# Two pairs of tokens instead of one group of four in the one-hot rows of the dense gates

## The chip, the core and the metric

The kernel runs on one core of a Trainium2 chip. The metric is device microseconds of one execution; lower is better. The unchanged kernel was run three times for its time, and once more with the hardware profiler.

## What is computed

The reference is two transformer blocks over 512 tokens of width 1024. The part that matters here is the PEER layer of the first block: eight heads each choose 16 of 16,384 experts for a token, and each chosen expert contributes `gate * v_e * gelu(u_e . x)`.

```python
def peer(h, wq, k1, k2, u, v):
    ...
    top_s, top_c = lax.top_k(cand, PEER_TOPK)
    expert = (i1[top_c // 16] * PEER_N_KEYS + i2[top_c % 16])      # 128 choices a token
    gate = jax.nn.softmax(top_s, axis=-1)
    ...
    act = gelu(einsum("pd,ped->pe", xb, u[eb]))
    return einsum("pe,ped->pd", gb * act, v[eb])
```

## The kernel before

For 448 of the 512 tokens (`DT`) the kernel does not gather experts. It computes `gelu(u_e . x)` for all 16,384 experts, multiplies by a dense table of gates that is zero where a token did not choose the expert, and multiplies by all `v_e`. The expert number is written as `a * 128 + b`, so a token's gates are a 128x128 matrix over (b, a), and that matrix is a product of one-hot matrices: for the 128 choices of one token (they lie on the partitions) row `b` one-hot is the stationary operand, row `a` one-hot times the gate is the moving operand, and TensorE sums over the choices. The gate is split into two f16 parts, so each token takes two accumulating products of 128x128 by 128x128.

Three tiles carry this, all f16. `hb` holds for each choice and token four numbers: a, b and the two gate parts. `iob` holds the numbers 0 to 127, each repeated. `oh` holds four tokens' one-hot rows: index 0 is a, index 1 is b, 2 and 3 are a's one-hot times the gate parts. For each group of four tokens VectorE makes `oh` in two instructions of 128x1024: an `is_equal` of `iob` with `hb` (L917, i = 0) and a product (L917, i = 2). Then TensorE makes eight products `pg` (L923), each with its own weight load, whose operands are the columns of one token in `oh`. In `oh` before, the four tokens are the innermost index, so one token's 128 elements stand 8 bytes apart. ScalarE copies the four tokens' result to `stg` (L924), and after 32 tokens `stg` goes to DRAM (`Gd`, 2 MB each, L926). There are 112 such groups, 896 products, and `oh` has two buffers.

This work is a generator, `router()`, whose steps are woven into the loop `for a in range(P)` over 128 tiles of experts. Each turn of that loop loads and splits a tile of `u` (`getw`: DMA to `wr`, ScalarE's cast to `wh` at L123, VectorE's rest `wl` at L124) and runs 24 products `pu` of 448 columns (L140 to L142). The loop also draws on `ada_step` (L264, VectorE rows over weights of the second block) and on `own_dots` (L945, VectorE dot products of gathered rows). How many steps of a generator come in a turn is set by the numbers they yield; every engine then executes its instructions in the order of the program. The dense-gate part takes some 42 turns and ends at a = 121; six turns later the loop over `peer_v` (`pvv`) follows.

Of the kernel before, what the change touches and what calls it, by code (L numbers as in the profile page):

```python
# [11 lines left out]
F16 = mybir.dt.float16  # L12
# [3 lines left out]
AF = mybir.ActivationFunctionType  # L16
OP = mybir.AluOpType
# [4 lines left out]
P = 128  # L22
D = 1024
T = 512
# [52 lines left out]
def body(tc, I, O, dbg=None):  # L77
    nc = tc.nc
    V, S, TE, G, SP = nc.vector, nc.scalar, nc.tensor, nc.gpsimd, nc.sync
    es = ExitStack()  # L80

    def pool(name, bufs=1, space=None, side=None, ctx=es):
        kw = {}
        if space is not None:
            kw["space"] = space
        if side is not None:
            kw["side"] = side
        return ctx.enter_context(tc.tile_pool(name=name, bufs=bufs, reuse_waits="tile", **kw))
# [24 lines left out]
    iota = ca[:, CA["iota"]:CA["iota"] + 128]  # L113
# [185 lines left out]
    with ExitStack() as e1:  # L299
# [121 lines left out]
        wk = pool("wk1", ctx=er)  # L421
# [6 lines left out]
        ps = gps.tile([P, 512], F32, tag="g", name="lps")[:, :4]  # L428
# [19 lines left out]
        def proj(n_ctx=True, lat=True):  # L448
            done = first.pop(0) if first else None
            wh, wl = done[0] if done else getw1(P)  # L450
            out = []
            if done:
                out.append(done[1])
            elif lat:
                ps = mm.tile([P, 512], F32, tag="mm", name="pj")
                mm_tiles([(ps, wh, wl)], H)
                out.append(ps)
            if n_ctx:
                pc = mm.tile([P, 512], F32, tag="mm", name="pjc")[:, :C]
                mm_tiles([(pc, wh, wl)], HC)  # L460
                out.append(pc)
            return out
# [181 lines left out]
        for p_ in range(4):  # L644
            vl, vc = proj_v()
            for hh in range(2):
                h = 2 * p_ + hh
                kf, lg = [], []
                for d in range(2):
                    _, f = sig_tile(proj(), Z_, KL)  # L650
                    i = d * 8 + h
# [20 lines left out]
        wk = pool("wk1g", ctx=er)  # L672
# [7 lines left out]
        for hh, at, n in ((H, 0, T), (HC, T, C)):  # L680
            ps = mm.tile([P, 512], F32, tag="mm", name="grp")[:32, :n]
# [3 lines left out]
        for h in range(4):  # L685
# [4 lines left out]
            for d in range(2):  # L690
                y_ = wk.tile([P, N2], F32, tag=KL[0], name="gz", bufs=KL[1])
                for at, n in ((0, T), (T, C)):
                    ps = mm.tile([P, 512], F32, tag="mm", name="gkp")[:, :n]
# [25 lines left out]
        wk = pool("wk1b", ctx=ey)  # L719
        yh = wk.tile([P, 2, 16, T], F32R, name="yh1")  # L720
        for i in range(16):
            t = wk.tile([P, T], F32, tag="yl", name="yl", bufs=2)
            SP.dma_start(t, ysd[i])
            split(yh[:, 0, i], yh[:, 1, i], t)
        for i in range(16):
            ps, = proj(n_ctx=False)
# [9 lines left out]
        for n in range(KT):  # L736
            acc = []
            ada_step(wk, row1, 4)
            for br in range(2):
# [3 lines left out]
                ps = mb.tile([P, 512], F32, tag="mm", name="br")  # L743
# [14 lines left out]
        for n in range(KT):  # L758
            wh, wl = getw1(P)
            ps = mb.tile([P, 512], F32, tag="mm", name="wo")  # L760
# [31 lines left out]
    with ExitStack() as e1:  # L792
# [3 lines left out]
        wk = wk2 = pool("wk2", ctx=e1)  # L796
# [6 lines left out]
        wk = wk2  # L803
# [4 lines left out]
        eall = wk.tile([P, 4, P], F32, name="eall")  # L808
        gall = wk.tile([P, 4, 8, 16], F32, name="gall")
        abg = rp.tile([P, T], F32, name="abg")  # L810
        hb = wk.tile([P, 4, T], F16, name="hb")
        iob = wk.tile([P, P, 4], F16, name="iob")
        hrow = rp.tile([P, 1024], F32, name="hrow")
        V.tensor_copy(iob, iota[:, :, None].to_broadcast([P, P, 4]))
        rows = {}
        for (i, j) in RANKS:
            rows[i] = rows.get(i, 0) + 1
# [9 lines left out]
        def router():  # L827
            for h in range(8):
                vs, xs = [], []
                for half in range(2):  # L830
                    wh, wl = getw(I["wq"][h * 2 + half], P)
                    ps = mm.tile([P, 512], F32, tag="mm", name="pq")
# [5 lines left out]
                    ps = gps.tile([P, 512], F32, tag="g", name="ps")  # L838
# [19 lines left out]
                for w, src in enumerate((vs, xs)):  # L858
                    at = 0
                    for i in range(8):  # L860
                        n = rows[i]
# [40 lines left out]
            for w, src in enumerate((abf[:, 0], abf[:, 1], gall.rearrange("p m h i -> p m (h i)"))):  # L902
                tp = gps.tile([P, 512], F32, tag="g", name="tpg")
                for m in range(4):
                    TE.transpose(tp[:, m * P:(m + 1) * P], src[:, m], ident)
                S.activation(abg, tp, AF.Copy, scale=2.0 ** 15) if w == 2 else S.copy(hb[:, w], tp)

            S.copy(hb[:, 2], abg)
            V.tensor_tensor(hb[:, 3], abg, hb[:, 2], op=OP.subtract)
            yield 0.7  # L910
            for tb in range(DT // TB):
                stg = wk.tile([P, P, TB], F32, tag="stg", name="stg", bufs=2)
                for t4 in range(TB // 4):
                    t = tb * TB + t4 * 4
                    oh = wk.tile([P, 4, P, 4], F16, tag="oh", name="oh", bufs=2)
                    for i in (0, 2):
                        V.tensor_tensor(oh[:, i:i + 2], (oh[:, 0] if i else iob)[:, None].to_broadcast([P, 2, P, 4]),  # L917
                                        hb[:, i:i + 2, None, t:t + 4].to_broadcast([P, 2, P, 4]),
                                        op=OP.mult if i else OP.is_equal)
                    ps = gps.tile([P, 512], F32, tag="g", name="pg").rearrange("p (t a) -> p t a", t=4)  # L920
                    for j in range(4):
                        for i in range(2):
                            TE.matmul(ps[:, j], oh[:, 1, :, j], oh[:, 2 + i, :, j], start=i == 0, stop=i == 1)  # L923
                    S.activation(stg[:, :, t4 * 4:t4 * 4 + 4], ps.rearrange("p t a -> p a t"), AF.Copy, scale=2.0 ** -15)  # L924
                    yield 1.4
                SP.dma_start(Gd[tb], stg.rearrange("p a t -> p (a t)"))  # L926
# [22 lines left out]
        NG, GA = 16, 8  # L949
        ready = [0]  # L950
        lane, mine = router(), own_dots()
        WORK = 8 * 36.2 + 4.7 + 1.4 * DT / 4 + 1.3 * NSL
        spent = n_own = 0.0
# [3 lines left out]
        for a in range(P):  # L957
            if first:
                ps = first.pop(0)[0]
            else:  # L960
                wh, wl = getw(I["peer_u"][a], P)
                ps = mm.tile([P, 512], F32, tag="mm", name="pu")[:, :DT]
                mm_tiles([(ps, wh, wl)], Hd)
            t = gl.tile([P, DT], F32, tag="gel", name="gel", bufs=4)
# [52 lines left out]
    with ExitStack() as e1:  # L1017
        mm = pool("mm2b", 6, PSUM, ctx=e1)
        wk = pool("wk3", ctx=e1)
# [4 lines left out]
        for g in range(NG):  # L1024
# [15 lines left out]
            for j in range(KT):  # L1040
                wh, wl = getw(I["peer_v"][g * KT + j], P)
                ps = mm.tile([P, 512], F32, tag="mm", name="pvv")[:, :DT]
# [3 lines left out]
                while n_own < NSL + LAG and n_own < (NSL + LAG) * (g * KT + j + 1) / ((NG - 2) * KT):  # L1046
                    if n_own < NSL:
                        vs.append(fetch(wk, I["peer_vr"], n_own, LAG))
                    if n_own >= LAG:
                        n = n_own - LAG  # L1050
# [64 lines left out]
    for l in range(2):  # L1115
# [20 lines left out]
        wk = pool(f"wk6{l}", side="right", ctx=ea)  # L1136
# [163 lines left out]
        for hf in range(2):  # L1300
            ws = [getw(next2(), 256) for _ in range(2)]
            for uu, nt, o0 in ((UC, 2, 0), (U, 4, 2)):
                for m in range(nt):
                    ps = mm.tile([P, 512], F32, tag="mm", name="pr2")[:, :256]
# [7 lines left out]
        for m in range(6):  # L1312
            if m % 2 == 0:
                ps2 = sps.tile([P, 1024], F32, tag="sp", name="pvb")
            ps = ps2[:, m % 2 * 512:m % 2 * 512 + 512]
# [6 lines left out]
        for t_ in range(4):  # L1322
            st_ = [ptile("kb_s", F32R) for _ in range(2)]
            ps = sps.tile([P, 1024], F32, tag="sp", name="pkb")
# [6 lines left out]
        for t_ in range(6):  # L1331
            if t_ % 3 == 0:
                uqs = getw(I["uq"][l, t_ // 3], P, 768)
            ps = sps.tile([P, 1024], F32, tag="sp", name="pqb")
            for a0 in range(0, NQ, 512):
                a1 = min(NQ, a0 + 512)
                for k in range(2):
                    i = (t_ % 3) * 2 + k
# [161 lines left out]
        for bi, (q0, m) in enumerate(blocks):  # L1500
# [4 lines left out]
            for g in range(2):  # L1505
                ws = []
                for r in range(4):
# [3 lines left out]
                    for c0, c1 in ((0, 256), (256 + lo_ * P, 256 + hi_ * P)):  # L1511
                        while c0 < c1:
                            n = min(c1 - c0, 512 - at % 512)
# [35 lines left out]
        with ExitStack() as e2:  # L1549
            mm = pool(f"mm6{l}", 8, PSUM, ctx=e2)  # L1550
            wk = pool(f"wk7{l}", side="right", ctx=e2)
            for n_ in range(3):
# [5 lines left out]
                for jp in range(4):  # L1558
                    wh, wl = getw(I[f"wb_{l}"][n_ * 4 + jp], P)
                    for jj in range(2):  # L1560
                        j = jp * 2 + jj
                        gt = wk.tile([P, NQ], F32, tag="yt", name="gt2", bufs=6)
                        SP.dma_start(gt, gd2[n_ * 8 + j, :, :NQ])
                        for a0, n in spans:
                            ps = mm.tile([P, 512], F32, tag="mm", name="pb")[:, :n]
# [37 lines left out]
        with ExitStack() as e2:  # L1603
            mm = pool(f"mm7{l}", 6, PSUM, ctx=e2)
            for j in range(KT):
                wh, wl = getw(I[f"wo_{l}"][j], P)
                for hh, a0, n, w in toks:
                    ps = mm.tile([P, 512], F32, tag="mm", name="pwo")[:, :n]
# [10 lines left out]
        with ExitStack() as e2:  # L1619
# [5 lines left out]
            wk = pool(f"wk8{l}", ctx=e2)  # L1625
# [262 lines left out]
```

## Time and profile before

| | |
|---|---|
| median of 3 runs | 4973.27 us (4970.96 to 4980.0) |
| profiled execution | 4975.9 us, span 4974.1 us |
| TensorE busy | 4832.7 us (97%) |
| VectorE busy | 3295.3 us (66%) |
| ScalarE busy | 1968.7 us (40%) |
| mean granted TensorE clock | 0.989 |
| dense gates (first to last `pg`) | 1514.7 to 1828.4 us of the span |

The profiled execution is 2.6 us above the median. The shares are means over many stages; the dense gates are 6% of the span, and only this stretch runs the changed instructions in number.

### The profile page before, as it was taken

The numbers are of one execution on the slowest core, as the hardware profiler recorded it, in microseconds if no ns is written. First come the engines' busy times: TensorE is split into PE (matmuls) and PEld (weight loads), VectorE is DVE, ScalarE is ACT, GpSimd is POOL, SyncE is SP. The second block draws the span as 40 slices with busy tenths as digits, with TensorE's granted clock in tenths as the row PEclk, the third lists the DMA queues.
The fourth block names the chain that finished last, engine by engine and source line by source line (L and its number), as shares of the span: only waits on it lengthen the run. The fifth ranks groups of instructions, "written<-read, shape, count | busy, mean of one in ns | idle before, by whom it ended". The sixth has DMA issues, their size and how long they took to land.

```text
span 4974.1 us, 67442 instructions
## 1 busy us (share of the span) xinstructions
PE 4832.7 (97%) x26062; PEld 4111.5 (83%) x26062; DVE 3295.3 (66%) x6062; ACT 1968.7 (40%) x3214; POOL 345.7 (7%) x352
## 2 busy tenths in 40 slices
PE   7999999999999999999999999999999999999999
PEld 6888888788888988999988768888888886677887
DVE  7665556688888866777658773268655568726655
ACT  4544445332233432333345553224222455533433
POOL 0000000001111103333000100000000001100000
PEclk9999999999999999999999999999999999999999
DMA  4211117656667778777534532444432245245332
GB/s 163 62 52 54 56 51 245 212 176 203 218 210 249 262 254 305 265 263 271 163 118 119 136 83 96 143 146 132 143 116 71 72 138 138 69 140 180 91 96 85
DMA packets 236676, 752.08 MB, mean 151 GB/s; under 512 B 27458, under 2 KB 55618, under 8 KB 233796
## 3 DMA queue, kind: packets, MB, share of 16 engines
q1 hardware_dynamic: 193156, 580.00, 35.8%
q0 software_dynamic: 43200, 167.79, 11.2%
q8 instruction: 204, 3.34, 0.3%
q14 instruction: 116, 0.95, 0.1%
HBM read 619.09 MB, written 123.35 MB: 149 GB/s over the span
## 4 chain that ended last, share of the span: by engine, by line
PE 84%; DVE 8%; DMA 4%; ACT 3%; issue 2%; POOL 0%; DVEq 0%; ACTq 0%; SPq 0%; POOLq 0%
PE pj L140 6%; PE pj L141 6%; PE pj L142 6%; PE pvv L140 4%; PE pup L140 4%; PE pvv L141 4%; PE pvv L142 4%; PE pup L142 4%; PE pup L141 4%; PE pu L142 3%; PE pu L140 3%; PE pu L141 3%; PE tp L1230 3%; PE pg L923 2%; PE pdn L140 2%; PE pdn L141 2%
## 5 line engine op out<-in xcount | busy, mean ns | idle before, releaser
L123 ACT CAST wh<-wr 128x1024 fp32r<-128x1024 f32 (+4 forms) x660 | 679.1, 1029 | 1610.8 <-PE pvv L141 370.1
L124 DVE TENSOR_TENSOR wl<-wr,wh 128x1024 fp32r<-128x1024 f32 (+4 forms) x660 | 788.7, 1195 | 678.4 <-ACT wh L123 661.7
L142 PE MATMUL pu<-H,wl 128*128 128x448 f32 x1024 | 382.8, 374 | 12.4 <-DVE wl L124 12.4
L140 PE MATMUL pvv<-W,wh 128*128 128x448 f32 x1024 | 376.5, 368 | 15.3 <-ACT W L123 15.3
L140 PE MATMUL pu<-H,wh 128*128 128x448 f32 x1024 | 383.4, 375 | 5.0 <-ACT H L223 3.0
L142 PE MATMUL pvv<-W,wl 128*128 128x448 f32 x1024 | 376.4, 368 | 3.5 <-DVE wl L124 3.5
L141 PE MATMUL pu<-H,wh 128*128 128x448 f32 x1024 | 378.9, 370 | 0.0
L140 PE MATMUL pup<-U,wh 128*128 128x512 f32 (+1 forms) x1056 | 374.1, 355 | 3.2 <-ACT U L223 3.0
L141 PE MATMUL pvv<-W,wh 128*128 128x448 f32 x1024 | 376.2, 368 | 0.1
L141 PE MATMUL pup<-U,wh 128*128 128x512 f32 (+1 forms) x1056 | 374.3, 355 | 0.0
L142 PE MATMUL pup<-U,wl 128*128 128x512 f32 (+1 forms) x1056 | 374.1, 354 | 0.2 <-DVE wl L124 0.2
L140 PE MATMUL pj<-U,wh 128*128 128x512 f32 (+1 forms) x672 | 267.6, 398 | 0.0
L141 PE MATMUL pj<-U,wh 128*128 128x512 f32 (+1 forms) x672 | 267.4, 398 | 0.0
L142 PE MATMUL pj<-U,wl 128*128 128x512 f32 (+1 forms) x672 | 265.5, 395 | 0.0
L140 PEld LDWEIGHTS pup<-U,wh 128*128 128x128 f32 x1056 | 200.0, 190 | 32.8 <-ACT U L223 4.2
L142 PEld LDWEIGHTS pup<-U,wl 128*128 128x128 f32 x1056 | 199.7, 189 | 28.8 <-DVE wl L124 0.6
L141 PEld LDWEIGHTS pup<-U,wh 128*128 128x128 f32 x1056 | 199.9, 189 | 27.7 <-DVE U L224 0.3
L142 PEld LDWEIGHTS pu<-H,wl 128*128 128x128 f32 x1024 | 195.4, 191 | 32.4 <-DVE wl L124 15.7
L140 PEld LDWEIGHTS pvv<-W,wh 128*128 128x128 f32 x1024 | 193.7, 189 | 31.4 <-ACT W L123 15.7
L140 PEld LDWEIGHTS pu<-H,wh 128*128 128x128 f32 x1024 | 195.7, 191 | 23.1 <-ACT H L223 4.5
L142 PEld LDWEIGHTS pvv<-W,wl 128*128 128x128 f32 x1024 | 193.8, 189 | 19.8 <-DVE wl L124 4.1
L141 PEld LDWEIGHTS pu<-H,wh 128*128 128x128 f32 x1024 | 195.1, 191 | 17.3 <-DVE H L224 0.4
(507 smaller groups left out, 11925.5 us busy)
## 6 DMA issues: line engine op xcount, KB each, us to landing
wr<-in_w_dram SPq DMA_DIRECT2D x146, 512.0 KB
wr<-in_peer_u_dram SPq DMA_DIRECT2D x128, 512.0 KB
wr<-in_peer_v_dram SPq DMA_DIRECT2D x128, 512.0 KB
wa<-in_ada2T_dram SPq DMA_DIRECT2D x96, 512.0 KB
wr<-in_up_dram SPq DMA_DIRECT2D x88, 512.0 KB
geld<-gel SPq DMA_DIRECT2D x128, 224.0 KB
Gd<-stg SPq DMA_DIRECT2D x14, 2048.0 KB
gt<-Gd POOLq DMA_DIRECT2D x32, 896.0 KB, 8.4
```

The costliest lines, as they stand in the source:

```text
L123: S.copy(hi, src)
L124: V.tensor_sub(lo, src, r32(hi))
L140: TE.matmul(ps, ah, bh, start=start, stop=False)
L141: TE.matmul(ps, ah, bl, start=False, stop=False)
L142: TE.matmul(ps, al, bh, start=False, stop=stop)
L923: TE.matmul(ps[:, j], oh[:, 1, :, j], oh[:, 2 + i, :, j], start=i == 0, stop=i == 1)
L1230: TE.transpose(tp[:, m * P:(m + 1) * P], w_[:, c0:c0 + P], ident)
```

## The change

In `oh` the four tokens of a group become two pairs: the order of the indices was (kind, n, token) and is now (kind, pair, n, token in the pair). A token's 128 elements then stand 4 bytes apart. `iob` repeats each number twice instead of four times, and `hb` is stored as (group of four tokens, kind, token), so that the two pairs of one or two kinds follow one another. The two VectorE instructions of a group keep their 1024 elements a partition; the innermost run of the `hb` operand is two elements instead of four. The products and their number are the same.

```diff
-        hb = wk.tile([P, 4, T], F16, name="hb")
-        iob = wk.tile([P, P, 4], F16, name="iob")
+        hb = wk.tile([P, T // 4, 4, 4], F16, name="hb")
+        iob = wk.tile([P, P, 2], F16, name="iob")
...
-        V.tensor_copy(iob, iota[:, :, None].to_broadcast([P, P, 4]))
+        V.tensor_copy(iob, iota[:, :, None].to_broadcast([P, P, 2]))
...
-                S.activation(abg, tp, AF.Copy, scale=2.0 ** 15) if w == 2 else S.copy(hb[:, w], tp)
-
-            S.copy(hb[:, 2], abg)
-            V.tensor_tensor(hb[:, 3], abg, hb[:, 2], op=OP.subtract)
+                S.activation(abg, tp, AF.Copy, scale=2.0 ** 15) if w == 2 else S.copy(hb[:, :, w], tp.rearrange("p (g t) -> p g t", t=4))
+
+            ag4 = abg.rearrange("p (g t) -> p g t", t=4)
+            S.copy(hb[:, :, 2], ag4)
+            V.tensor_tensor(hb[:, :, 3], ag4, hb[:, :, 2], op=OP.subtract)
...
-                    oh = wk.tile([P, 4, P, 4], F16, tag="oh", name="oh", bufs=2)
+                    oh = wk.tile([P, 4, 2, P, 2], F16, tag="oh", name="oh", bufs=2)
                     for i in (0, 2):
-                        V.tensor_tensor(oh[:, i:i + 2], (oh[:, 0] if i else iob)[:, None].to_broadcast([P, 2, P, 4]),
-                                        hb[:, i:i + 2, None, t:t + 4].to_broadcast([P, 2, P, 4]),
-                                        op=OP.mult if i else OP.is_equal)
+                        row = hb[:, t // 4, i:i + 2].rearrange("p w (u v) -> p (w u) v", v=2)
+                        dst = oh[:, i:i + 2].rearrange("p w u n v -> p (w u) n v")
+                        if i == 0:
+                            V.tensor_tensor(dst, iob[:, None].to_broadcast([P, 4, P, 2]),
+                                            row[:, :, None].to_broadcast([P, 4, P, 2]), op=OP.is_equal)
+                        else:
+                            V.tensor_tensor(oh[:, 2:4], oh[:, 0, None].to_broadcast([P, 2, 2, P, 2]),
+                                            hb[:, t // 4, 2:4].rearrange("p w (u v) -> p w u v", v=2)[:, :, :, None].to_broadcast([P, 2, 2, P, 2]),
+                                            op=OP.mult)
...
-                            TE.matmul(ps[:, j], oh[:, 1, :, j], oh[:, 2 + i, :, j], start=i == 0, stop=i == 1)
+                            TE.matmul(ps[:, j], oh[:, 1, j // 2, :, j % 2], oh[:, 2 + i, j // 2, :, j % 2], start=i == 0, stop=i == 1)
```

No engine's instructions change place. This is VectorE where the dense gates begin, before the change (`aj,sdot` are the dot products of `own_dots`, `aj,ac` those of `ada_step`):

```order
L917 TENSOR_TENSOR oh<-iob,hb 128x1024 x2
L124 TENSOR_TENSOR wl<-wr,wh 128x1024
L909 TENSOR_TENSOR hb<-abg,hb 128x512
L917 TENSOR_TENSOR oh<-oh,hb 128x1024 x2
L945 SCALAR_TENSOR_TENSOR aj,sdot<-ut,hrow 128x1024
L917 TENSOR_TENSOR oh<-iob,hb 128x1024 x2
L917 TENSOR_TENSOR oh<-oh,hb 128x1024 x2
L264 SCALAR_TENSOR_TENSOR aj,ac<-wa,rows_u_8239 128x1024
```

And the same place with the change:

```order
L922 TENSOR_TENSOR oh<-iob,hb 128x1024 x2
L124 TENSOR_TENSOR wl<-wr,wh 128x1024
L910 TENSOR_TENSOR hb<-abg,hb 128x128x4
L925 TENSOR_TENSOR oh<-oh,hb 128x1024 x2
L953 SCALAR_TENSOR_TENSOR aj,sdot<-ut,hrow 128x1024
L922 TENSOR_TENSOR oh<-iob,hb 128x1024 x2
L925 TENSOR_TENSOR oh<-oh,hb 128x1024 x2
L264 SCALAR_TENSOR_TENSOR aj,ac<-wa,rows_u_8239 128x1024
```

Only line numbers and the shape of the `hb` operand differ; on TensorE, GpSimd and SyncE no operand shape differs either, on ScalarE the three copies to `hb` do, on VectorE also the copy to `iob`.

## Rows read from the trace of the kernel before

**Rows 1.** The page, its busy times and its chain that ended last.
```profile
PE 4832.7 (97%) x26062; PEld 4111.5 (83%) x26062; DVE 3295.3 (66%) x6062; ACT 1968.7 (40%) x3214; POOL 345.7 (7%) x352
...
PE 84%; DVE 8%; DMA 4%; ACT 3%; issue 2%; POOL 0%; DVEq 0%; ACTq 0%; SPq 0%; POOLq 0%
```

**Rows 2.** Busy time by stretch, dense gates: stretch, us, engines, PEclk, DMA share, GB/s.
```profile
1515.00:1555.00 40.00, 40.00 (x247) 35.95 (x245) 33.68 (x53) 17.19 (x27) 5.50 (x4) 1.00 0.70 240
...
1675.00:1715.00 40.00, 40.00 (x247) 36.09 (x246) 32.13 (x52) 15.89 (x25) 4.15 (x4) 1.00 0.80 278
...
1795.00:1829.00 34.00, 34.00 (x214) 30.45 (x213) 26.34 (x38) 15.36 (x24) 0.00 (x0) 1.00 0.57 202
sum 314.00, PE 314.00 PEld 281.73 DVE 256.08 ACT 127.09 POOL 29.01; mean PE 39.25 PEld 35.22 DVE 32.01 ACT 15.89 POOL 3.63
```

**Rows 3.** Line L923, the gate products: ns min/median/max, first and last start.
```profile
L923 PEld LDWEIGHTS <-oh x896: 112/117/141, 1514.7 to 1828.0; 128*128 128x128 f16 x180
L923 PE MATMUL pg<-oh x896: 283/297/302, 1514.7 to 1828.1; 128*128 128x128 f16 x180
```

**Rows 4.** The chain from 1602 to 1612 us: start, us, what.
```profile
1602.52 1.90 PE pg L923 x16
1604.42 0.21 PE pu L140
...
1606.25 0.20 PE pu L140
1606.45 0.96 PE pg L923 x8
1607.41 0.21 PE pu L141
```

**Rows 5.** Line L1520, products of 128 columns that lie 4 bytes apart.
```profile
L1520 PEld LDWEIGHTS spc<-maskr x96: 187/190/192, 2920.1 to 4350.1; 128*128 128x128 f32 x96
L1520 PE MATMUL spc<-maskr x96: 220/230/307, 2920.2 to 4350.2; 128*128 128x128 f32 x96
```

**Rows 6.** Timeline of PE around 2881 us: products of 256 columns back to back.
```profile
2880.61 0.29 PE L140 MATMUL pj<-UC,wh 128*128 128x256 f32 x1
2880.74 0.28 PE L141 MATMUL pj<-UC,wh 128*128 128x256 f32 x1
...
2881.21 0.28 PE L142 MATMUL pj<-UC,wl 128*128 128x256 f32 x1
```

**Rows 7.** Groups by line and shape on VectorE, 1515 to 1829 us: busy, mean ns, idle.
```profile
L917 DVE TENSOR_TENSOR oh<-iob,hb 128x1024 f16<-128x1024 f16 x110 | 75.8, 691 | 57.4 <-PE pg L923 57.1
L917 DVE TENSOR_TENSOR oh<-oh,hb 128x1024 f16<-128x1024 f16 x111 | 73.8, 687 | 0.3
L124 DVE TENSOR_TENSOR wl<-wr,wh 128x1024 fp32r<-128x1024 f32 x43 | 52.3, 1221 | 0.0
```

**Rows 8.** Who waited for whom, 1515 to 1829 us: total us, times, longest.
```profile
DVE oh L917 <- PE pg L923: 57.1, 74, 2.8
...
PEld L923 <- DVE oh L917: 6.1, 28, 0.2
ACT wh L123 <- DMA wr<-in_peer_u_dram: 3.0, 1, 3.0
```

**Rows 9.** Busy time by stretch, before and behind the dense gates (columns as Rows 2).
```profile
1200.00:1300.00 100.00, 94.41 (x455) 84.82 (x454) 93.35 (x268) 27.46 (x37) 15.55 (x12) 0.98 0.70 219
...
1829.00:1900.00 71.00, 55.70 (x260) 50.15 (x259) 34.08 (x52) 20.54 (x33) 11.26 (x13) 0.88 0.92 332
```

**Rows 10.** Groups by line, 1505 to 1515 us: the work that fills `hb` once.
```profile
L906 ACT CAST hb<-tpg 128x512 f16<-128x512 f32 x2 | 1.1, 586 | 0.0
...
L909 DVE TENSOR_TENSOR hb<-abg,hb 128x512 f16<-128x512 f32 x1 | 0.7, 684 | 0.0
L908 ACT CAST hb<-abg 128x512 f16<-128x512 f32 x1 | 0.6, 641 | 0.0
```

## The prediction

> **What bounds the kernel now.** I read the page first. TensorE is busy for 97% of the span and holds 84% of the chain that ended last [rows 1], so a change counts if it shortens what TensorE does, or if it makes another engine late enough to stop TensorE. The changed instructions stand almost wholly between 1514.7 and 1828.4 us, so I read that stretch by itself. [...] The reader is to see two things there: TensorE sets the pace, and VectorE is not far behind, at 82%.
>
> Who waits for whom says the same. VectorE's idle time is nearly all the wait of the first `oh` instruction until a gate product has let go of its buffer, 57.1 us in 74 waits; TensorE waited for `oh` 6.1 us in 28 waits, each of which is the short step at the head of a burst (0.2 us at most), and a late tile of `u` cost one wait of 3.0 us on ScalarE [rows 8]. So VectorE and the DMAs are ahead, and TensorE's own instructions are what the stretch is made of.
>
> How much of it are the gate products? In the chain 16 of them take 1.90 us, eight take 0.96 [rows 4]. That is 0.1188 us for one, with its weight load, and 896 of them [rows 3] take 106.4 us. The stretch is 313.7 us long, so the other products, mostly `pu` at about 0.21 us [rows 4], hold 207.3 us.
>
> **The reads of TensorE.** The change alters one thing for TensorE: the distance of the 128 elements that it reads as stationary and as moving operand, 8 bytes before and 4 after. What does a 128-column product cost at 4 bytes? No f16 product of that kind is in the trace, but there are products of fp32r data, whose elements are 4 bytes apart and neighbours. One of 128 columns takes 220 ns at least and 230 in the median [rows 5]; a gate product of the same 128 columns takes 283 at least and 297 in the median [rows 3]. The gate product is 63 to 67 ns longer. A second row says how large a stream that is: fp32r products of 256 columns follow one another at 120 ns (2880.61 to 2881.21 us, five steps) [rows 6]. The gate products, with half as many columns, go at 118.8. So a column at 8 bytes costs what two columns cost at 4.
>
> To turn the duration into a pace I need what lies between them. Products of 256 columns last 280 ns and follow at 120, so 160 of a duration overlap with the next product [rows 6]; gate products last 297 and follow at 118.8, so 178 do. From 220 to 230 ns that gives 42 to 70 ns. The lower figure leaves nothing for the weight load, so I take 66 ns, near the upper. The other end is 117 ns, the weight load's own duration [rows 3], if that and not the stream is what the next product waits for (a rival below). But an fp32r weight load takes 190 ns [rows 5] while products with such loads follow at 120 [rows 6], so a load's recorded duration can be longer than the pace; this is why I go by the stream.
>
> At 66 ns the 896 products take 59.1 us and TensorE needs 207.3 + 59.1 = 266.4 us for the stretch, 47.3 less than now.
>
> **VectorE's part.** The two instructions of a group keep 1024 elements. An f16 instruction of this size takes 691 ns and 687, an fp32 one of the same size (`wl`) 1221 [rows 7]: the f16 ones handle two elements in the time of one, and 530 ns an instruction hang on that. Before, the `hb` operand has runs of four elements, now of two. Between 687 (runs of two go as fast) and 1221 (they go one by one) I take 687 to 691: the destination is as contiguous as before, and runs of four show no price: an instruction with an fp32 source and 512 elements takes 684 ns [rows 10], the f16 ones with 512 pairs 687 and 691, so 128 or 256 runs cost 7 ns at most. [...]
>
> Then VectorE needs 256.1 us, and TensorE 266.4. Two engines that feed one another through two `oh` buffers and three of `wl` do not both reach 100%. The busiest long stretch of VectorE in this loop is 1200 to 1300 us: it is busy 93.35% there, TensorE 94.41% [rows 9]. If VectorE reaches 92.5% the stretch is 256.1 / 0.925 = 277 us long, and TensorE then works 96% of it. The ends are 266.4 us (VectorE never late) and 266.4 / 0.9441 = 282 us (TensorE as idle as in that row). I take 277: 36.7 us less than 313.7. What is late next is then `oh` itself: TensorE's weight load waits for VectorE at the head of a burst, where it did not wait before in earnest.
>
> **The edits with no price.** The copy to `iob` halves its elements, and the four instructions that fill `hb` write runs of four instead of whole rows. They run once and take 0.6 to 0.7 us each [rows 10], under the `pu` products; if the cover were gone and each took twice its time, it would be under 3 us. The order on every engine is as before, so no wait moves to another queue, and ScalarE's `stg` (L924) has the same form.
>
> **The sum.** 4975.9 us for the profiled execution, less 36.7, is 4939.2; that execution was 2.6 us above the median, so I expect 4936.6, say 4937 us.
>
> **The rivals.**
>
> *The distance is not what the gate products pay for: no change.* The next gate product begins where the weight load's 117 ns end, and 117 is also the pace [rows 3, 4]. If the load is the pace and keeps it, the stretch stays 313.7 us and the time 4973. If only the load gets a little shorter, to 108, it is 896 x 9 ns = 8 us, which is still no change that can be told. Against it speaks that the product itself, counted from after its load, lasts 63 to 67 ns longer than one of 128 columns at 4 bytes. [...]
>
> *The gain is made and given back: no change.* Behind the gates the DMA engines are 92% busy at 332 GB/s [rows 9], and TensorE waits. If an earlier end only lengthened that wait, nothing would be left. For this the gates' own traffic would have to be the cause; its stretches run at shares of 0.57 to 0.80 [rows 2], and 313.7 / 277 of the highest is 0.91, just under the 0.92 that the chip carries there. The loads behind are started by buffers that come free earlier as well.
>
> *VectorE loses its double rate: slower.* If runs of two go one element at a time, each of the 224 instructions takes 1221 ns instead of 689, 119 us more. VectorE then needs 375 us where it had 313.7, TensorE waits, and the stretch is 375 us at least and 386 at 97% busy: 61 to 72 us more, 5035 to 5046 us. Faster reads of TensorE would change nothing then. The point from which this decides is 58 us more on VectorE, or 0.26 us an instruction (0.95 us each); from there the stretch is longer than now whatever TensorE does. If it hits only one of the two instructions, VectorE needs 316 us, and the time is 4975 to 4985. For it speaks that the trace has no two-byte operand with runs of two; against it, that runs of four show no price at all.
>
> **How the numbers follow.** The three runs differ by 9 us, so 0.2%, 10 us, is about what a measurement of this kernel can tell from no change. I give the forecast 0.74. Its own range is 4927 (TensorE at 266.4 us, all 47 us saved) to 4946: a pace of 80 ns makes TensorE need 279 us, and with the stops of a VectorE at 90 to 92% the stretch 283 to 286, so 28 to 31 us saved. The no-change rivals have 0.15 together, of which giving back has 0.04, and end at 4965 to 4977. The slower rival has 0.11. To leave out no more than 2 in 10 the range must take in the no-change case, so it goes from 4927 to 4976. Faster by over 0.2% is the forecast, 0.74; within 0.2% is 0.15; slower 0.11.
>
> **What would show it.** In the changed kernel's profile the gate products should last some 230 ns and 16 of them should take about 1.1 us in the chain. The `oh` instructions should stay at 690 ns. The gates should last about 277 us, VectorE's wait for gate products should fall from 57 us to about 15, and waits of TensorE for `oh` should grow to some 10 us. The stretches before and behind should keep their lengths. I am wrong if the products stay at 297 ns (then the distance is not the price), if `oh` instructions near 1.2 us appear (then VectorE sets the pace), or if the gates shorten and the `peer_v` loop starts no earlier.

## The result and the profile after

The changed kernel takes 4918.82 us (median of 4 runs, 4916.02 to 4925.45) against 4976.64 us (4 runs beside it, 4970.96 to 4990.23). The ratio is 0.9885, with a 95% interval of [0.9869, 0.9901]: 58 us faster, where some 37 were forecast, and 8 us below the lower end of the range. The profiled execution took 4916.02 us with a span of 4914.3 us.

The page of the changed kernel, busy times and the chain, answers to [rows 1]. The shares are the same to within a per cent; TensorE's busy time is 60.7 us shorter, the span 59.8.

```profile
PE 4772.0 (97%) x26062; PEld 4057.4 (83%) x26062; DVE 3288.9 (67%) x6062; ACT 1965.2 (40%) x3214; POOL 345.0 (7%) x352
...
PE 84%; DVE 8%; DMA 4%; ACT 3%; issue 2%; POOL 0%; SPq 0%; DVEq 0%; ACTq 0%; POOLq 0%
```

The line of the gate products, now L931 (ns min/median/max, first and last start), answers to [rows 3]. The median falls from 297 to 218 ns, the weight load from 117 to 97.

```profile
L931 PEld LDWEIGHTS <-oh x896: 96/97/103, 1512.9 to 1775.1; 128*128 128x128 f16 x180
L931 PE MATMUL pg<-oh x896: 217/218/234, 1512.9 to 1775.2; 128*128 128x128 f16 x180
```

The chain from 1745 to 1753 us (start, us, what) answers to [rows 4]: 16 products in 0.94 us, so 58.8 ns each where it was 118.8.

```profile
1745.29 0.47 PE pg L931 x8
1745.76 0.25 PE pu L140
...
1748.84 0.94 PE pg L931 x16
1749.78 0.25 PE pu L140
```

Busy time by stretch for the gates (stretch, us, engines, granted clock, DMA share, GB/s) answers to [rows 2]. TensorE is still busy throughout, and VectorE has gone from 82% (256.08 of 314.00 us) to 95% (248.64 of 262.00). The gates, from first to last product, shrink from 313.7 to 262.5 us.

```profile
1513.00:1775.00 262.00, 261.65 (x1902) 232.11 (x1901) 248.64 (x382) 120.92 (x195) 28.78 (x22) 1.00 0.84 304
```

Who waited for whom in this stretch answers to [rows 8], and the groups on VectorE to [rows 7]. VectorE's wait for `oh` buffers is down from 57.1 to 10.9 us, TensorE's for `oh` only up from 6.1 to 8.5, and the one-hot instructions (L922, L925) kept their length.

```profile
ACT wh L123 <- DMA wr<-in_peer_u_dram: 13.8, 8, 4.7
DVE oh L922 <- PE pg L931: 10.9, 16, 2.2
PEld L931 <- DVE oh L925: 8.5, 34, 0.5
```

```profile
L925 DVE TENSOR_TENSOR oh<-oh,hb 128x1024 f16<-128x1024 f16 x111 | 73.7, 686 | 0.3
L922 DVE TENSOR_TENSOR oh<-iob,hb 128x1024 f16<-128x1024 f16 x110 | 72.8, 687 | 11.2 <-PE pg L931 10.9
L124 DVE TENSOR_TENSOR wl<-wr,wh 128x1024 fp32r<-128x1024 f32 x42 | 51.0, 1220 | 1.7 <-ACT wh L123 1.7
```

So 51.2 of the 59.8 us between the two profiles were won in the gates, 1.8 before them and 6.8 behind. The 1.8 us lie within the scatter: over the profiles of this document the gates begin anywhere from 1503.2 to 1515.5 us, and the profile of kernel 8, which is the changed kernel again, has them begin at 1514.7 as before the change.

### The profile page after: what moved, and what is told of

Its sections match the earlier page's. It is cut to its first block, busy times and chain, and to the rows that moved or that the text cites. A ratio compares the mean times of both kernels' runs of the same rounds, so it can differ in the third digit from the quotient of the medians.

```text
span 4914.3 us, 67442 instructions
## 1 busy us (share of the span) xinstructions
PE 4772.0 (97%) x26062; PEld 4057.4 (83%) x26062; DVE 3288.9 (67%) x6062; ACT 1965.2 (40%) x3214; POOL 345.0 (7%) x352
## 4 chain that ended last, share of the span: by engine, by line
PE 84%; DVE 8%; DMA 4%; ACT 3%; issue 2%; POOL 0%; SPq 0%; DVEq 0%; ACTq 0%; POOLq 0%
PE pj L141 6%; PE pj L140 6%; PE pj L142 6%; PE pup L140 4%; PE pup L142 4%; PE pvv L140 4%; PE pup L141 4%; PE pvv L141 4%; PE pvv L142 4%; PE pu L142 3%; PE pu L140 3%; PE pu L141 3%; PE tp L1238 3%; PE pdn L140 2%; PE pdn L141 2%; PE pdn L142 2%
## 5 line engine op out<-in xcount | busy, mean ns | idle before, releaser
L141 PE MATMUL pj<-H,wh 128*128 128x512 f32 x512 | 208.2, 407 | 0.0
```

The lines of the kernel that those rows point to most:

```text
L141: TE.matmul(ps, ah, bl, start=False, stop=False)
```

## Experiments

Two questions stand: is it the distance, and of which operand; and why did the gates end at 262.5 us and not at 277? A theory for the first is that the distance of the moving operand's elements sets the pace of the products, the further apart the slower. Its rivals are the weight load, and a part won by VectorE or the new order of `hb`.

**1. Both operands at 8 bytes again, all else changed (w8m8).** A view that takes every fourth element of the changed tile:

```diff
+        def far(ap, j):
+            return ap.rearrange("p u n v -> p (u n v)").rearrange("p (n k) -> p n k", k=4)[:, :, j]
...
-                            TE.matmul(ps[:, j], oh[:, 1, j // 2, :, j % 2], oh[:, 2 + i, j // 2, :, j % 2], ...
+                            TE.matmul(ps[:, j], far(oh[:, 1], j), far(oh[:, 2 + i], j), ...
```

> The changed tiles and VectorE instructions, but TensorE reads every fourth element again, so both operands lie 8 bytes apart. (The products mix columns of two pairs, so the gate table's values are not the reference's; number and size of all instructions are the same.) Theory, the distance is the whole of the gain: gate products at 297 ns, 118.8 ns apart in the chain, the gates 312 to 315 us long, time 4970 to 4982 us, as before the change. Rival, VectorE's new form or the new order of hb gained a part: time 4935 to 4965 us, with the gates clearly under 310 us.

The time is 4976.68 us, ratio to before 1.0012 [0.9996, 1.0027]. The gates run from 1503.2 to 1816.8 us, 313.7 us as before. Its product line:

```profile
L934 PEld LDWEIGHTS <-oh x896: 112/117/141, 1503.2 to 1816.4; 128*128 128x128 f16 x180
L934 PE MATMUL pg<-oh x896: 283/297/303, 1503.2 to 1816.5; 128*128 128x128 f16 x180
```

The gain in the gates hangs wholly on the distance at which TensorE reads. The new tiles, runs of two and all, gain and cost nothing that this run can tell by themselves.

**2 and 3. One operand at 8 bytes (w8m4 the stationary, w4m8 the moving).** `far` is used for one of the two operands.

> Changed kernel with only the stationary operand read at 8 bytes, the moving one at 4 (values of the gate table are mixed up, work is the same). Theory A, the moving stream sets the pace: products about 220 ns, 58 to 62 ns apart, the gates 262 to 267 us, time 4917 to 4928 us. Rival B, the weight load sets it: loads at 117 ns, products 118 ns apart, the gates 313 us, time 4970 to 4982 us. Rival C, each operand pays its share: products some 85 to 95 ns apart, the gates 285 to 295 us, time 4943 to 4957 us.

> Changed kernel with only the moving operand read at 8 bytes, the stationary one at 4 (values of the gate table are mixed up, work is the same). Theory A, the moving stream sets the pace: products about 297 ns and 116 to 119 ns apart though the weight load is at 97 ns, the gates 310 to 314 us, time 4968 to 4982 us. Rival B, the weight load sets it: products 57 to 60 ns apart, the gates 263 us, time 4917 to 4928 us. Rival C, both pay: 85 to 95 ns apart, time 4943 to 4957 us.

With the stationary operand at 8 bytes: 4924.3 us, ratio to before 0.9911 [0.9893, 0.9929], the gates 264.2 us, 16 products in 0.98 us. With the moving one: 4978.84 us, ratio 1.0008 [0.9996, 1.0021], the gates 311.0 us, 16 in 1.87 us. The product lines and a line of the chain from 1740 to 1755 us (start, us, what), w8m4 first and then w4m8:

```profile
L934 PEld LDWEIGHTS <-oh x896: 111/113/137, 1514.2 to 1778.1; 128*128 128x128 f16 x180
L934 PE MATMUL pg<-oh x896: 217/221/253, 1514.2 to 1778.2; 128*128 128x128 f16 x180
...
1745.15 0.98 PE pg L934 x16
```

```profile
L934 PEld LDWEIGHTS <-oh x896: 96/115/119, 1515.5 to 1826.1; 128*128 128x128 f16 x180
L934 PE MATMUL pg<-oh x896: 277/296/300, 1515.5 to 1826.2; 128*128 128x128 f16 x180
...
1748.38 1.87 PE pg L934 x16
```

The moving operand's distance is nearly all of it; the stationary one's is worth some 2 ns a product. The load's recorded 113 ns in w8m4 go with a pace of 61 ns: a load's duration is not the pace. In w4m8 the load has 4-byte data and still shows 115 ns at the median, so that duration does not follow the stationary operand's distance alone; that it reflects the stream beside it is my reading.

**4. Six distances in one kernel (steps).** The groups take six lines of products in turn, each line with its own distance from 2 to 16 bytes, for both operands:

```diff
+        def apart(ap, d, j):
+            return ap.rearrange("p w u n v -> p (w u n v)")[:, :P * d].rearrange("p (n k) -> p n k", k=d)[:, :, j % d]
...
+                            if (t // 4) % 6 == 0:
+                                TE.matmul(ps[:, j], apart(oh[:, 0:2], 1, j), apart(oh[:, 2:4], 1, j), ...
+                            elif (t // 4) % 6 == 1:
+                                TE.matmul(ps[:, j], apart(oh[:, 0:2], 2, j), apart(oh[:, 2:4], 2, j), ...
...
+                            elif (t // 4) % 6 == 5:
+                                TE.matmul(ps[:, j], apart(oh[:, 0:2], 8, j), apart(oh[:, 2:4], 8, j), ...
```

Two readings are told apart by it: L, a price that grows with the distance beyond 4 bytes, and H, one price for every distance beyond 4.

> Changed kernel in which each sixth group of four tokens has its products read at another distance, both operands, 2, 4, 6, 8, 12 and 16 bytes, each on its own line (the gate table's values are not the reference's; number and size of the instructions are the same). [...] Rival H, anything over 4 bytes takes half rate and no more: 297 ns at 6, 8, 12 and 16. [...] Time between the one before and the one after for H, 4945 to 4960 us; for L about 4965 to 4980 us.

One run took 4978.12 us. The lines of the products in its chain, around 1550 us (start, us, what), at 2 bytes (L935), 4 (L937), 6 (L939), 8 (L941), 12 (L943) and 16 (L945):

```profile
1544.44 0.46 PE pg L935 x8
...
1548.21 0.47 PE pg L937 x8
1548.68 0.69 PE pg L939 x8
...
1554.26 0.96 PE pg L941 x8
1555.21 1.38 PE pg L943 x8
...
1558.22 1.90 PE pg L945 x8
```

One product takes 58, 59, 86, 120, 173 and 238 ns, with median durations of 219, 218, 252, 298, 353 and 413. The 128 elements at 6, 8, 12 and 16 bytes span 768, 1024, 1536 and 2048 bytes: 0.112, 0.117, 0.112 and 0.116 ns a byte. The price of distance thus grows in proportion from 6 to 16 bytes, as L has it, and H falls: 12 and 16 bytes (173 and 238 ns) cost far more than 8 (120), and 6 bytes (86) already cost half as much again as 4 (59). What in the reads makes this price is not shown, and no kernel here has distances over 16 bytes. Nor are the operands told apart here; kernels 2 and 3 do that for 8 bytes only. From 2 to 4 bytes nothing changes (58 and 59 ns), so a distance of 2 bytes would have given no more than the pairs do.

**5. Half of TensorE's gate products (half).** The second product of each token, with the smaller part of the gate, is left out.

```diff
-                        for i in range(2):
-                            TE.matmul(ps[:, j], ..., oh[:, 2 + i, j // 2, :, j % 2], start=i == 0, stop=i == 1)
+                        TE.matmul(ps[:, j], ..., oh[:, 2, j // 2, :, j % 2], start=True, stop=True)
```

> Changed kernel without the second product of each token (the smaller part of the gate is left out), so 448 gate products instead of 896; VectorE's work is whole. TensorE then needs about 26 us less, 236 to 238 us, and VectorE 249 to 256 us. Theory, VectorE can work at 97% and more beside TensorE, so that the ceiling of 92.5% in the prediction was the wrong step: the gates take 252 to 260 us, VectorE is busy 97 to 100% of them, TensorE idles or waits 15 us and more. Rival, VectorE does have a ceiling near 92 to 95% and the 262.5 us of the changed kernel are already set by it: the gates stay at 260 to 270 us. Time 4906 to 4918 us by the theory, 4914 to 4930 by the rival.

4921.18 us (one run), the gates 258.7 us. The busy times from 1515 to 1750 us and the waits from 1513 to 1775:

```profile
1515.00:1750.00 235.00, 219.63 (x1311) 187.07 (x1310) 222.59 (x343) 109.25 (x175) 27.24 (x22) 0.99 0.85 306
```

```profile
ACT wh L123 <- DMA wr<-in_peer_u_dram: 43.9, 21, 4.8
...
PEld L930 <- DVE oh L925: 15.2, 54, 1.5
PEld pu L140 <- ACT wh L123: 8.4, 5, 3.4
PEld pu L142 <- DVE wl L124: 7.5, 7, 1.5
...
DVE wl L124 <- ACT wh L123: 5.5, 5, 2.5
...
DVE oh L922 <- PE pg L930: 5.0, 2, 4.5
```

My theory, that VectorE can work at 97% and more, falls: it stays at 94.7%. Of the 26 us taken from TensorE the gates shrink by only 4. TensorE waits for `oh`, for `wl` and for `wh`, and ScalarE's `wh` waits 43.9 us for tiles of `u`. The length lies at the theory's upper end, but time and share are the rival's. There is a second limit close under the first. It is not VectorE alone: of its 12.4 idle us in the stretch the greater part are waits for `wh`, which is behind the tiles of `u`, and for gate products. How much of the 258.7 us VectorE sets and how much the tiles is not told apart.

**6. VectorE relieved (less_dve).** The second instruction of each group is left out, and the products read the one-hot row without the gate.

```diff
-                    for i in (0, 2):
+                    for i in (0,):
...
-                            TE.matmul(ps[:, j], ..., oh[:, 2 + i, j // 2, :, j % 2], start=i == 0, stop=i == 1)
+                            TE.matmul(ps[:, j], ..., oh[:, 0, j // 2, :, j % 2], start=i == 0, stop=i == 1)
```

> Changed kernel without the second VectorE instruction of each group (the products read the plain one-hot row instead of the one times the gate, so the gates are left out), 77 us less for VectorE, TensorE's work whole. Theory, TensorE alone sets the length of the gates in the changed kernel: they take 254 to 262 us and the time is 4908 to 4924 us. Rival, VectorE at 95 to 98% holds TensorE back by more than the 9 us of waits that the profile shows: the gates take under 250 us, time under 4905 us.

4922.27 us (one run), and the gates take 262.7 us, a little over the 254 to 262 expected. Taking 77 us from VectorE gains nothing: in the changed kernel TensorE alone sets the length of the gates, and it is busy 253.55 of 255 us here. The busy times and VectorE's wait show that the relief went into waiting:

```profile
1515.00:1770.00 255.00, 253.55 (x1841) 226.30 (x1840) 176.82 (x261) 114.13 (x190) 28.72 (x21) 1.00 0.85 309
```

```profile
DVE oh L922 <- PE pg L931: 66.7, 26, 3.4
```

**7. No runs for VectorE (runs_of_none).** Made from the kernel before: the token is outermost, TensorE reads neighbours, and each value of `hb` repeats 128 times.

```diff
-        iob = wk.tile([P, P, 4], F16, name="iob")
+        iob = wk.tile([P, P], F16, name="iob")
...
-                    oh = wk.tile([P, 4, P, 4], F16, tag="oh", name="oh", bufs=2)
+                    oh = wk.tile([P, 4, 4, P], F16, tag="oh", name="oh", bufs=2)
                     for i in (0, 2):
-                        V.tensor_tensor(oh[:, i:i + 2], (oh[:, 0] if i else iob)[:, None].to_broadcast([P, 2, P, 4]),
-                                        hb[:, i:i + 2, None, t:t + 4].to_broadcast([P, 2, P, 4]),
+                        V.tensor_tensor(oh[:, i:i + 2], (oh[:, 0, None] if i else iob[:, None, None]).to_broadcast([P, 2, 4, P]),
+                                        hb[:, i:i + 2, t:t + 4, None].to_broadcast([P, 2, 4, P]),
...
-                            TE.matmul(ps[:, j], oh[:, 1, :, j], oh[:, 2 + i, :, j], ...
+                            TE.matmul(ps[:, j], oh[:, 1, j], oh[:, 2 + i, j], ...
```

> The one-hot rows with the token outermost: TensorE reads 2 bytes apart, and the hb operand of VectorE's instructions has no run, each value repeats 128 times. The result is the reference's. Theory of the slower rival: without a run of at least two elements the two-byte instructions lose their double rate and take about 1220 ns; VectorE needs 375 us, the gates take 375 to 390 us, time 5030 to 5050 us although a gate product costs 56 ns. Other: a repeated element keeps the rate, 690 ns, gates 260 to 263 us, time 4912 to 4925 us.

5031.53 us (one run), the gates 385.7 us. The one-hot instructions, the busy times and TensorE's wait for `oh`:

```profile
L917 DVE TENSOR_TENSOR oh<-iob,hb x112: 1214/1219/1227, 1499.2 to 1886.0; 128x1024 f16<-128x1024 f16 x112
L917 DVE TENSOR_TENSOR oh<-oh,hb x112: 1214/1218/1224, 1503.2 to 1888.3; 128x1024 f16<-128x1024 f16 x112
```

```profile
1520.00:1880.00 360.00, 291.44 (x1764) 244.10 (x1761) 337.80 (x350) 117.18 (x182) 35.32 (x21) 0.86 0.60 209
```

```profile
PEld L923 <- DVE oh L917: 44.0, 49, 4.1
```

This is the slower rival as it was priced (1221 ns, 375 to 386 us). A run of two keeps the double rate (687 and 686 ns in the changed kernel), a repeated single element does not (1219 and 1218). Here VectorE is the busiest engine, at 94%, and TensorE waits for it.

**8. The changed kernel once more (after_again).**

> The changed kernel once more, unaltered, to see what of the 60 us between the two profiles lies in the gates and what is scatter. Theory: the gates take 262 to 264 us again, the rest behind them 3139 to 3151 us as in the other profiles (scatter), median 4918 to 4926 us. Rival: the rest behind the gates is 3139 us again, some 7 us under the kernels with products at 8 bytes, and so a second gain of the change.

4924.9 us (4 runs), ratio to before 0.9893 [0.987, 0.9915]. The gates take 262.1 us. From the last product's start to the end of the span it is 3138.9 us, as in the first profile (3139.1); before it was 3146.0. The others lie at 3145.6 (w8m8), 3142.2 (w8m4), 3151.7 (w4m8), 3148.0 (steps), 3146.7 (half), 3144.4 (less_dve) and 3139.5 (runs_of_none). So kernels whose moving operand lies at 4 bytes or less spread from 3139 to 3147 and the others from 3146 to 3152. The two profiles of the change agree with the rival, the kernels 5 and 6 with scatter; this is not settled. A closer look at the loop over `peer_v` leans to the rival. Its second sixteenth, from the first of its 192 products to the first of the next, takes 43.7 to 47.8 us in the four profiles with moving operands over 4 bytes (before, w8m8, w4m8 and, in part, steps) and 39.0 to 43.4 in the other six. The two groups lie apart, though only just, and no run here tells why.

## Why the prediction was too small

The direction and the mechanism, that the distance of the reads is what the gate products pay for, were right; the size was not, because the step from TensorE's need to the length of the gates failed. Between the profiles the forecast of 36.7 us is 23.1 short of the 59.8 measured: 14.5 us in the gates (277 forecast, 262.5 measured: 10.6 by the length that was put on top of TensorE's need and 4 by that need) and 8.6 outside them, where nothing was forecast. Step by step:

- **TensorE sets the pace in the gates.** Right, before and after; kernel 6 shows it for after.
- **A column at 8 bytes costs two at 4, and it is the reads of the stream that cost.** Right, by kernels 1 to 4: 118.8 ns a product at 8 bytes, 58.8 at 4. Kernels 2 and 3 show that the moving operand pays: 16 products take 0.98 us with the stationary one at 8 bytes and 1.87 with the moving one.
- **66 ns a product.** Mis-sized: 58.8 ns. The f16 product lasts 218 ns where fp32r rows of 220 to 230 stood in for it, and 218 - 58.8 = 159 ns of it overlap with the next, as in the fp32r row (160) and not as in the gate products before (178). I went "near the upper" end of 42 to 70 ns to leave room for the weight load, and it needed none beyond this. This is 896 x 7.2 ns = 6.5 us. TensorE's need of 266.4 us becomes 260, and what remains of the stretch, the other products, is 2.5 longer (209.8 us instead of 207.3); the first `pu` behind a burst takes 0.25 us in the chain where it took 0.21.
- **The length of 277 us, 256.1 / 0.925.** This is the step that failed. I let VectorE's pauses set the length and so put 10.6 us on top of TensorE's need of 266.4. No such pauses came: TensorE was busy 261.65 of 262 us, its weight loads waited for `oh` in 34 steps of at most 0.5 us, and with VectorE relieved of 77 us the gates kept their length (kernel 6). Of the two numbers, the divisor was not far from what VectorE reaches where it is the busiest engine (94.7% in kernel 5, 94% in kernel 7), although the row it came from [rows 9] had another cause, as the waits from 1200 to 1300 us of the kernel before show: ScalarE stood 25.3 + 14.9 us for tiles from DRAM, and TensorE for `wl` behind it.

```profile
ACT wh L123 <- DMA wr<-in_peer_u_dram: 25.3, 8, 8.4
ACT wh L123 <- DMA wr<-in_wq_dram: 14.9, 3, 5.9
...
DVE wl L124 <- ACT wh L123: 6.1, 4, 5.0
PEld pu L142 <- DVE wl L124: 5.9, 3, 3.4
```

  The dividend was too large: VectorE was busy 248.6 us in the changed gates, not 256.1. Busy time is not a fixed need. In the timeline of the kernel before, around 1605 us, one `oh` instruction that follows a pause takes 0.69 us and two in a row 1.29, so neighbours overlap by some 0.09 us in the record:

```profile
1604.46 0.69 DVE L917 TENSOR_TENSOR oh<-iob,hb 128x1024 f16<-128x1024 f16 x1 [0.26 <-PE pg L923]
1605.07 1.29 DVE L917 TENSOR_TENSOR oh<-oh,hb 128x1024 f16<-128x1024 f16 x2
```

  With 58 pauses fewer (74 before, 16 after) there are 58 more such overlaps, some 5 us of busy time, and one `wl` and one `ada_step` row less stand inside the new stretch, 2.4 us. Together that is the 7.5 us by which 256.1 was too large. In the measured 262 us VectorE is 94.9% busy, about the share at which it topped out in kernels 5 and 7, and TensorE's own need lies there too: the two limits nearly meet, and kernel 6 shows that TensorE's is the higher. The range's lower end, "VectorE never late", was the true case; it was set too high by the 66 ns, and nothing was added for the stretches outside the gates. (Its sum, 4975.9 - 47.3 - 2.6, gives 4926 and not 4927.)
- **VectorE keeps its double rate.** Right: 687 and 686 ns with runs of two. Kernel 7 shows that the slower rival had its price right (1219 ns), only not its condition: it takes a single repeated element.
- **The edits with no price.** Right within what kernel 1 can tell (its gates are as long as before).
- **The stretches before and behind keep their length.** They gave 8.6 us between the two profiles, a term that the sum put at nothing. The 1.8 us before the gates are within the scatter. Behind the gates the difference lies early in the loop over `peer_v`. Its second sixteenth (192 products) takes 46.0 us before and 40.5 after. These are the busy times of the two stretches. TensorE stands idle 3.6 us in the first and 1.0 in the second, and its mean granted clock is 0.93 in the first and 1.00 in the second:

```profile
1915.00:1961.00 46.00, 42.40 (x194) 38.24 (x193) 33.81 (x46) 12.61 (x17) 16.82 (x11) 0.93 0.77 269
```

```profile
1863.20:1903.70 40.50, 39.48 (x193) 35.97 (x193) 30.02 (x40) 12.54 (x17) 14.86 (x10) 1.00 0.84 294
```

  Whether that belongs to the change stays open (kernel 8).

The rivals: the distance not being paid for falls by kernel 1, where the products at 8 bytes last 297 ns and the gates 313.7 us as before. Giving back did not happen: the DMA engines carried the denser gates at a share of 0.84.

## What to carry to other kernels

Look at TensorE's operands in bytes, not only in shapes: with 16-bit operands 4 bytes from element to element, a product of 128 columns went at 59 ns, as at 2 bytes (58), and at 6 or 8 bytes it took 86 or 120; a layout that leaves VectorE runs of two (687 ns for 1024 elements) and TensorE 4 bytes serves both. When the leading engine gets faster, do not add the pauses of the second engine onto it from a row elsewhere without reading what those pauses waited for, and do not take the second engine's busy time beside pauses for its need. Two one-sided runs, one engine relieved and then the other, tell which of two close limits is the higher.

## What the runs showed of the hardware that was not expected

With both operands at the same distance, a product's time grew with the bytes that 128 elements span, some 0.11 to 0.12 ns for each of 768 to 2048 bytes, and stayed at 58 to 59 ns for 256 and 512. At 8 bytes it was the moving operand that paid: the stationary operand's distance changed the recorded weight load (97 ns at 4 bytes, 113 to 117 at 8, 146 at 16 with both operands there) but at 8 bytes the pace only by 2 ns. With VectorE as the busiest engine (kernel 7) TensorE was busy 291.44 of 360 us, with waits for `oh` of up to 4.1 us, and its mean granted clock in the gates was 0.86; in the changed kernel it was 1.00. On VectorE a two-byte operand with a run of two kept the double rate (687 ns for 1024 elements), and a single element repeated did not (1219 ns).
